# The second product of an MLP as seven block products, with sums of weight blocks made ahead

## The chip, the cores and the metric

The kernel runs on one core of a Trainium2 chip. It is written against the core's engines directly: TensorE (PE) multiplies matrices into PSUM, VectorE (DVE), ScalarE (ACT) and GpSimd (POOL) work on tiles element by element, SyncE (SP) issues the DMAs. The metric is the time of one execution on the device, in microseconds; lower is better. Times given as the median are over three runs.

## The reference

Two decoder layers over 512 tokens of 1024 features. Each layer has an attention mixer, then a squared-ReLU MLP with 4096 hidden features, then a gate from an embedding:

```python
hn = rms(h, g_mlp_pre[i])
y = jnp.square(jax.nn.relu(hn @ w_mlp_in[i])) @ w_mlp_out[i]
h = h + rms(y, g_mlp_post[i])
gate = jax.nn.sigmoid(h @ w_ple_gate[i])
h = h + gate * (p[i] @ w_ple_proj[i])
```

`hn @ w_mlp_in` is 512x1024 by 1024x4096, the product with `w_mlp_out` 512x4096 by 4096x1024, the gate 512x1024 by 1024x1024. All data is float32.

## The kernel before

Each float32 operand is split into a high part (a cast to a shorter type, by ScalarE) and a low part (what is left, by VectorE or GpSimd), and each product is three matmuls, high by high, high by low, low by high (`mm3`, L200 to 209). Weights come through one stream (`Stream`, L127 to 163): a 128x1024 piece is loaded by SyncE into `raw` (four buffers), cast into `wh` and subtracted into `wl` (four each). A piece is prepared when an earlier one is freed, and SyncE runs one queue in program order.

The code that the change touches is `layer_tail`, the MLP and gate of a layer, called once per layer:

1. The first product (`z`, L834 to 876) yields the hidden features transposed, 32 tiles `a` of 128 features by 512 tokens. Each takes 24 matmuls of 512 columns into one PSUM bank, then VectorE (into a tile with the tag `t`, which has two buffers) and ScalarE make the squared ReLU of it, scaled, in `at`.
2. The second product (`y`, L884 to 919) has eight PSUM banks, four rows of 128 tokens by two halves of 512 output features. In each of 32 rounds `k` one tile `a` is split into `ah` and `al`, and `mm3` is done for all eight banks: 24 matmuls. The last four rounds (`TAIL`) are held and then done row by row: after a row's matmuls VectorE, ScalarE and GpSimd form its norm and update the residual `h` (`post_norm`, L306), and the row before it is transposed (`pre_transpose`, `transpose_rows`, L233) for the gate.
3. The gate product (`pj` into `proj`, L251) reads these transposed rows (tiles `big`, named `hg`) and the stream's `w_g`; the low part of a transposed row is written by VectorE at L249.

The order in which each engine gets its instructions is that in which the Python code issues them, with a scheduler that may move an instruction ahead of others on its engine where no data forbids it. In the lists below a name with a number is one buffer of a tile.

Of the kernel before, what the change touches and what calls it, by code (L numbers as in the profile page):

```python
# [10 lines left out]
F32 = mybir.dt.float32  # L11
# [7 lines left out]
P = 128  # L19
# [26 lines left out]
TAIL = 4  # L46
# [12 lines left out]
def trunk_kernel(ctx, tc, A, out):  # L59
# [15 lines left out]
    def bank(tag, name):  # L75
        return psum.tile([P, 512], F32, tag=tag, name=name)
# [13 lines left out]
    def f32(ap):  # L90
        return ap.bitcast(F32)


    hspill = nc.dram_tensor("h_spill_dram", (NR, P, D), F32, kind="Internal").ap()
    ples = nc.dram_tensor("ple_dram", (2, NR, P, D), F32, kind="Internal").ap()
# [26 lines left out]
    class Stream:  # L122
# [22 lines left out]
        def load(self, upto):  # L145
            while len(self.raws) <= min(upto, len(self.specs) - 1):
                src, n, _ = self.specs[len(self.raws)]
                raw = ring.tile([P, 1024], F32, tag="raw", bufs=RAW, name="raw")
                sync.dma_start(raw[:, :n], src)
                self.raws.append(raw)  # L150
# [23 lines left out]
    for i in range(2):  # L174
# [20 lines left out]
        for j in range(KF):  # L195
            ws.add(A[f"w_mo{i}"][j], 1024)
# [615 lines left out]
    def layer_tail(i, p0, og, oT, hts, last, begin=None):  # L812
        gi = 4 * i
        with tc.tile_pool(name=f"tail{i}", bufs=1) as mp:
# [51 lines left out]
            for fb in range(NB):  # L866
                if fb:
                    z_part(*first[fb], 256, 512)
                ws.free()
                z_evac(fb, first[fb][0])  # L870
            for fb in range(NB, KF):
                h, l = ws.next()
                ps = bank("A", "z")
                z_part(ps, h, l, 0, 512)
                ws.free()
                z_evac(fb, ps)

# [6 lines left out]
            acc = [[None] * 2 for _ in range(NR)]  # L884
            for r in range(NR):
                for n in range(2):
                    acc[r][n] = bank("AB"[n], f"y{r}{n}")
            tailk = []

            def y_mm(r, n, ah, al, h, l, k):  # L890
                c = slice(r * P, (r + 1) * P)
                w = slice(n * 512, (n + 1) * 512)
                mm3(acc[r][n], ah[:, c], al[:, c], h[:, w], l[:, w], k == 0, k == KF - 1)

            for k in range(KF):
                h, l = ws.next()
                ah = mp.tile([P, S], F32R, tag="ah", bufs=5, name="ah")
                al = mp.tile([P, S], F32R, tag="al", bufs=5, name="al")
                src = at[k // 4][:, k % 4, :]
                act.copy(ah, src)  # L900
                pool.tensor_tensor(al, src, f32(ah), op=ALU.subtract)  # L901
                if k < KF - TAIL:
                    for r in range(NR):
                        for n in range(2):
                            y_mm(r, n, ah, al, h, l, k)
                    ws.free()
                else:
                    tailk.append((ah, al, h, l, k))
            new_big()
            xg = make_xt([0, 1], [2, 3], KD, f"hg{i}")  # L910
            ssy = keep(8)
            for r in range(NR):
                for ah, al, h, l, k in tailk:
                    for n in range(2):
                        y_mm(r, n, ah, al, h, l, k)
                if r:
                    pre_transpose(mp, r - 1, None, xg)
                post_norm(mp, r, acc[r], gpost, ssy)
            ws.free(TAIL)

# [13 lines left out]
            def gate0(r, ps):  # L934
                gate(r, ps, 0)
                if r == 1:
                    pre_transpose(mp, 3, None, xg)
# [16 lines left out]
            drain(proj(xg, 512, [2] * 4, range(NR), gate0))  # L954
# [337 lines left out]
```

## Time and profile before

| what | value |
|---|---|
| median of three runs | 1355.7 us (1354.56 to 1356.21) |
| the profiled execution | 1353.69 us |
| its span, first to last instruction | 1351.9 us |
| TensorE busy (matmul) | 1329.3 us, 98% |
| weight loads of TensorE | 1117.6 us, 83% |
| VectorE busy | 708.1 us, 52% |
| ScalarE busy | 574.1 us, 42% |
| GpSimd busy | 261.3 us, 19% |
| DMA | 135.39 MB, mean 100 GB/s |

Busy times of different engines overlap, so they do not add up to the span. A busy TensorE is no proof that it works at full rate: the bars of matmuls overlap in the pipeline (each is drawn longer than the time by which it advances the queue), so the rate is read from the distance between starts, or from a count over a stretch. The profile also lists a granted clock of TensorE, 1.00 at full speed.

### The profile page before, as it was taken

How to read it: one execution, taken by the hardware profiler on the slowest of the kernel's cores; microseconds unless marked ns; L12 is line 12 of the kernel's file. 1: busy time of each engine (PE TensorE's matmuls, PEld its weight loads, DVE VectorE, ACT ScalarE, POOL GpSimd, SP SyncE). 2: the span in 40 equal slices, each digit the busy share in tenths (PEclk: the TensorE clock that was granted, in tenths of full speed). 3: DMA queues.
4: the chain of work that ended last, by engine and by line, in shares of the span. 5: the costliest groups of instructions: out<-in, count | busy, mean ns of one | idle time of the engine just before them, and what ended most of it. 6: DMA issues, size and time to landing. Idle time of an engine off the chain costs nothing.

```text
span 1351.9 us, 17863 instructions
## 1 busy us (share of the span) xinstructions
PE 1329.3 (98%) x6809; PEld 1117.6 (83%) x6809; DVE 708.1 (52%) x1297; ACT 574.1 (42%) x1113; POOL 261.3 (19%) x233
## 2 busy tenths in 40 slices
PE   9999989999999999999998999999999999999998
PEld 6888878898888888888897679998988888888887
DVE  6678676473333322225568999965633332222263
ACT  4245576353322223224346768854422232222332
POOL 4212101031000022222012744411400001222120
PEclk9999989999999999999999999999999999999999
DMA  7312232333333433332243341011433334333321
GB/s 288 107 63 71 63 125 73 131 116 119 94 94 95 157 104 96 94 94 84 87 151 102 110 119 39 1 64 63 141 94 97 105 94 156 94 95 104 98 78 48
DMA packets 40838, 135.39 MB, mean 100 GB/s; under 512 B 4656, under 2 KB 5808, under 8 KB 40752
## 3 DMA queue, kind: packets, MB, share of 16 engines
q1 hardware_dynamic: 40752, 134.24, 31.1%
q8 instruction: 54, 0.88, 0.3%
q14 instruction: 32, 0.26, 0.1%
HBM read 125.83 MB, written 8.39 MB: 99 GB/s over the span
## 4 chain that ended last, share of the span: by engine, by line
PE 87%; DVE 8%; ACT 2%; POOL 1%; issue 1%; DMA 1%; SPq 0%; POOLq 0%; DVEq 0%; ACTq 0%
PE z L201 26%; PE y L201 26%; PE pj L201 21%; PE sc L201 3%; PE pv L201 3%; DVE work L1123 2%; PE trp L361 2%; DVE m L1122 2%; PE ak L201 1%; PE ple L201 1%; PE tr L242 1%; POOL wl L141 1%; DVE wl L141 1%; PE trq L381 1%; DMA xraw<-in_xT_dram 1%
## 5 line engine op out<-in xcount | busy, mean ns | idle before, releaser
L141 DVE TENSOR_TENSOR wl<-raw,wh 128x1024 fp32r<-128x1024 f32 (+3 forms) x190 | 249.1, 1316 | 276.9 <-ACT wh L137 275.1
L137 ACT CAST wh<-raw 128x1024 fp32r<-128x1024 f32 (+3 forms) x206 | 212.2, 1034 | 282.1 <-issue 184.8
L201 PE MATMUL y<-wh,ah 128*128 128x512 f32 x512 | 199.6, 390 | 0.0
L201 PE MATMUL y<-wh,al 128*128 128x512 f32 x512 | 199.2, 389 | 0.0
L201 PE MATMUL y<-wl,ah 128*128 128x512 f32 x512 | 199.2, 389 | 0.0
L201 PE MATMUL pj<-wh,big 128*128 128x512 f32 (+1 forms) x444 | 148.5, 386 | 0.0
L846 DVE SCALAR_TENSOR_TENSOR t<-z,rb 128x512 f32<-128x512 f32 x64 | 44.2, 691 | 186.9 <-PE z L201 186.9
L201 PEld LDWEIGHTS y<-wh,ah 128*128 128x128 f32 x512 | 96.1, 188 | 19.9
L201 PEld LDWEIGHTS y<-wl,ah 128*128 128x128 f32 x512 | 96.1, 188 | 19.8
L201 PEld LDWEIGHTS y<-wh,al 128*128 128x128 f32 x512 | 96.1, 188 | 19.8
L901 POOL TENSOR_TENSOR al<-big,ah 128x512 fp32r<-128x512 f32 x24 | 32.5, 1359 | 383.3 <-ACT ah L900 383.3
L201 PE MATMUL z<-hz0H,wl 128*128 128x512 f32 (+1 forms) x288 | 105.4, 366 | 0.6 <-DVE wl L141 0.6
L201 PE MATMUL z<-hz0H,wh 128*128 128x512 f32 (+1 forms) x288 | 105.5, 366 | 0.2 <-ACT hz0H L248 0.2
L201 PE MATMUL z<-hz1H,wh 128*128 128x512 f32 (+1 forms) x288 | 105.5, 366 | 0.2 <-ACT hz1H L248 0.2
L201 PE MATMUL z<-hz1L,wh 128*128 128x512 f32 (+1 forms) x288 | 105.4, 366 | 0.3 <-DVE hz1L L249 0.3
L201 PE MATMUL z<-hz0L,wh 128*128 128x512 f32 (+1 forms) x288 | 105.4, 366 | 0.3 <-DVE hz0L L249 0.3
L201 PE MATMUL z<-hz1H,wl 128*128 128x512 f32 (+1 forms) x288 | 105.3, 365 | 0.0
L201 PEld LDWEIGHTS pj<-wh,big 128*128 128x128 f32 x444 | 82.9, 188 | 17.5 <-issue 0.7
L900 ACT CAST ah<-a 128x512 fp32r<-128x512 f32 x40 | 24.8, 621 | 154.7 <-PE y L201 154.7
L901 POOL TENSOR_TENSOR al<-a,ah 128x512 fp32r<-128x512 f32 x40 | 51.7, 1292 | 165.9 <-ACT ah L900 165.9
L209 POOL TENSOR_TENSOR st<-st,mhalf 128x1 f32<-128x1 f32 (+1 forms) x41 | 27.9, 682 | 225.4 <-DVE st L312 115.6
L201 PEld LDWEIGHTS z<-hz0H,wl 128*128 128x128 f32 x288 | 54.3, 189 | 9.4 <-DVE wl L141 0.8
(598 smaller groups left out, 2640.6 us busy)
## 6 DMA issues: line engine op xcount, KB each, us to landing
raw<-in_w_mi_dram SPq DMA_DIRECT2D x64, 512.0 KB, 3.7
raw<-in_w_mo_dram SPq DMA_DIRECT2D x64, 512.0 KB, 3.6
raw<-in_w_ab_dram SPq DMA_DIRECT2D x20, 512.0 KB, 4.9
raw<-in_w_g_dram SPq DMA_DIRECT2D x16, 512.0 KB, 3.7
raw<-in_w_oab_dram SPq DMA_DIRECT2D x8, 512.0 KB, 4.3
ple<-ple_dram SPq DMA_DIRECT2D x8, 512.0 KB, 5.7
raw<-in_w_oc_dram SPq DMA_DIRECT2D x8, 512.0 KB, 3.6
xr<-in_x_dram SPq DMA_DIRECT2D x4, 512.0 KB, 9.5
```

What stands on the lines that cost most here:

```text
L137: act.copy(h[:, :n], raw[:, :n])
L141: (pool if e == "p" else vec).tensor_tensor(l[:, c], raw[:, c], f32(h[:, c]), op=ALU.subtract)
L201: pe.matmul(ps, a, b, start=first, stop=last, skip_group_check=True)
L209: pool.tensor_tensor(dst, src, mhalf[:, :n], op=ALU.pow)
L242: pe.transpose(ps[:, i * P : (i + 1) * P], src(k), ident)
L361: pe.transpose(ps[:, i * P : (i + 1) * P], pt[:, OFF[qt] + kt * P : OFF[qt] + (kt + 1) * P], ident)
L381: pe.transpose(ps[:, r * P : (r + 1) * P], rows(r), ident)
L846: vec.scalar_tensor_tensor(t, ps, 0.0, rb, op0=ALU.max, op1=ALU.mult)
L900: act.copy(ah, src)
L901: pool.tensor_tensor(al, src, f32(ah), op=ALU.subtract)
L1122: vec.max(m8, w)
L1123: vec.match_replace(w, m8, w, MARK)
```

## The change

The second product is computed on 2x2 blocks: the tokens in two halves, pairs of 128 hidden features, the outputs in two halves. Seven products of blocks (numbered 1 to 7), made of sums and differences of blocks, take the place of eight. They are done in two passes over the 16 pairs, since a product needs two PSUM banks (two rows of 128 tokens): in the first pass products 5, 7, 1 and 6, in the second 2, 3 and 4. A piece of the weight stream serves 24 matmuls in the first pass per two pieces, and 36 per three in the second.

- The sums of weight blocks are made while the first product runs (`block_sums`): four blocks of 128x512 are loaded, GpSimd subtracts four times, and four blocks are stored to a DRAM tensor `tsum`, from which the stream reads them later. This is done 16 times per layer; the tiles share the tags `ah` and `al`.
- The sums of activation blocks (`sm`, tag `t`, and in place in `a`) are made by VectorE in front of each pair, 256 columns each. The low parts of activations are now VectorE's; GpSimd made them before.
- After the first pass, ScalarE and VectorE copy and add the eight banks into tiles `d` in SBUF, so that the banks are free for the second.
- The last group of the second pass is done one half of the rows after the other. Each half then gives two rows (`r` and `r + 2`), whose norms are formed from SBUF, and four rows of transposes follow.
- The rows of the gate product are taken in the order 0, 2, 1, 3.

Line numbers of the new code lie 8 to 10 lower in the file up to the first product; L857 is the line that was L846, L142 is L141, L260 is L249, L321 to L328 are L310 to L317.

```diff
@@ -92,6 +91,8 @@
     hspill = nc.dram_tensor("h_spill_dram", (NR, P, D), F32, kind="Internal").ap()
+    tsum = nc.dram_tensor("tsum_dram", (2, KF // 2, 2, P, D), F32, kind="Internal").ap()
     ples = nc.dram_tensor("ple_dram", (2, NR, P, D), F32, kind="Internal").ap()
     ident = const.tile([P, P], F32, name="ident")
     gpre0 = const.tile([P, KD], F32, name="gpre0")
@@ -146,7 +147,11 @@
             while len(self.raws) <= min(upto, len(self.specs) - 1):
                 src, n, _ = self.specs[len(self.raws)]
                 raw = ring.tile([P, 1024], F32, tag="raw", bufs=RAW, name="raw")
-                sync.dma_start(raw[:, :n], src)
+                if isinstance(src, list):
+                    for q, piece in enumerate(src):
+                        sync.dma_start(raw[:, q * 512 : (q + 1) * 512], piece)
+                else:
+                    sync.dma_start(raw[:, :n], src)
                 self.raws.append(raw)
         def next(self):
@@ -192,8 +197,14 @@
             ws.add(A["w_oc" if i else "w_oab"][j], 1024)
         for j in range(KF):
             ws.add(A[f"w_mi{i}"][j], 1024, Z_ENG[j])
-        for j in range(KF):
-            ws.add(A[f"w_mo{i}"][j], 1024)
+        wo, lo, hi = A[f"w_mo{i}"], slice(0, 512), slice(512, 1024)
+        for j in range(KF // 2):
+            ws.add(tsum[i, j, 0], 1024)
+            ws.add([wo[2 * j][:, lo], tsum[i, j, 1][:, hi]], 1024)
+        for j in range(0, KF // 2, 2):
+            ws.add(wo[2 * j + 1], 1024)
+            ws.add([tsum[i, j + q, 1][:, lo] for q in range(2)], 1024)
+            ws.add(wo[2 * j + 3], 1024)
         for j in range(8):
             ws.add(A[f"w_g{i}"][j], 1024, G_ENG[j])
@@ -868,12 +879,30 @@
                     z_part(*first[fb], 256, 512)
                 ws.free()
                 z_evac(fb, first[fb][0])
+            def block_sums(j):
+                b = [[mp.tile([P, 512], F32, tag=("ah", "al")[q], bufs=5, name="b") for n in range(2)] for q in range(2)]
+                c = [slice(0, 512), slice(512, 1024)]
+                for q in range(2):
+                    for n in range(2):
+                        sync.dma_start(b[q][n], A[f"w_mo{i}"][2 * j + q][:, c[n]])
+                (b11, b12), (b21, b22) = b
+                for d, x, y in ((b11, b12, b11), (b12, b22, b12), (b22, b22, b11), (b21, b22, b21)):
+                    pool.tensor_tensor(d, x, y, op=ALU.subtract)
+                for q in range(2):
+                    for n in range(2):
+                        sync.dma_start(tsum[i, j, q][:, c[n]], b[q][n])
             for fb in range(NB, KF):
+                if fb % 2 == 0:
+                    block_sums(fb // 2 - 2)
                 h, l = ws.next()
                 ps = bank("A", "z")
                 z_part(ps, h, l, 0, 512)
                 ws.free()
                 z_evac(fb, ps)
+            for j in range(KF // 2 - 2, KF // 2):
+                block_sums(j)
             pls = [slot(4 + q, f"ple{q}").rearrange("p (r d) -> p r d", d=D) for q in range(2)]
             for r in range(NR):
@@ -881,42 +910,117 @@
             gpost = gtile(mp, gi + 2, "gpost2")
             gnext = None if last else gtile(mp, gi + 3, "gnext")
...
+            NP = KF // 2
+            L, R = slice(0, 256), slice(256, 512)
+            x = [[at[j // 2][:, j % 2 * 2 + q, :] for q in range(2)] for j in range(NP)]
+            def part_tiles():
+                return [mp.tile([P, S], F32R, tag=nm, bufs=5, name=nm) for nm in ("ah", "al")]
+            def split(parts, c, src):
+                h, l = parts
+                act.copy(h[:, c], src)
+                vec.tensor_tensor(l[:, c], src, f32(h[:, c]), op=ALU.subtract)
+            def banks(ps):
+                return {p: [bank("AB"[r], f"y{p}{r}") for r in range(2)] for p in ps}
+            def mul(ps, r, a, qa, w, qw, first, last):
+                ca, cw = slice(qa * 256 + r * P, qa * 256 + (r + 1) * P), slice(qw * 512, (qw + 1) * 512)
+                mm3(ps[r], a[0][:, ca], a[1][:, ca], w[0][:, cw], w[1][:, cw], first, last)
+            acc = banks((5, 7, 1, 6))
+            held = []
+            def one(j, r, ops):
+                for p, a, qa, w, qw in ops:
+                    mul(acc[p], r, a, qa, w, qw, j == 0, j == NP - 1)
+            for j in range(NP):
+                x1, x2 = x[j]
+                sm = mp.tile([P, S], F32, tag="t", bufs=2, name="sm")
+                vec.tensor_tensor(sm[:, L], x1[:, R], x2[:, R], op=ALU.add)
+                vec.tensor_tensor(sm[:, R], x1[:, L], x1[:, R], op=ALU.subtract)
+                vec.tensor_tensor(x1[:, R], sm[:, L], x1[:, L], op=ALU.subtract)
+                a, a1 = part_tiles(), part_tiles()
+                split(a, slice(0, S), sm)
+                split(a1, slice(0, S), x1)
+                w = ws.next()
+                ops = [(5, a, 0, w, 0), (7, a, 1, w, 1)]
+                if j < NP - 2:
+                    for r in (1, 0):
+                        one(j, r, ops)
+                    ws.free()
+                w = ws.next()
+                ops1 = [(1, a1, 0, w, 0), (6, a1, 1, w, 1)]
+                if j < NP - 2:
+                    for r in (1, 0):
+                        one(j, r, ops1)
                     ws.free()
                 else:
+                    held.append((j, ops + ops1))
+            dt = []
+            for r in range(2):
+                for j, ops in held:
+                    one(j, r, ops)
+                d = slot(hts[2 + r], f"d{r}")
+                dt.append([d[:, q * 512 : (q + 1) * 512] for q in range(4)])
+            for r in range(2):
+                d11, d12, d21, c22 = dt[r]
+                act.copy(d11, acc[1][r])
+                for d, b, p in ((d21, d11, 6), (d12, d21, 5), (d21, d21, 7), (c22, d21, 5)):
+                    vec.tensor_tensor(d, acc[p][r], b, op=ALU.add)
+            ws.free(4)
+            acc = banks((2, 3, 4))
+            for j in range(0, NP, 2):
+                ac, a4 = [], part_tiles()
+                for q in range(2):
+                    x1, x2 = x[j + q]
+                    vec.tensor_tensor(x1[:, R], x2[:, L], x1[:, R], op=ALU.subtract)
+                    if q == 1:
+                        split(a4, R, x1[:, R])
+                    else:
+                        split(a4, L, x1[:, R])
+                    ac.append(part_tiles())
+                    split(ac[q], slice(0, S), x2)
+                ops = []
+                w0, w4, w1 = ws.next(), ws.next(), ws.next()
+                for q, w in ((0, w0), (1, w1)):
+                    ops.append([(2, ac[q], 0, w, 0), (3, a4, q, w, 1)])
+                ops4 = [[(4, ac[q], 1, w4, q)] for q in range(2)]
+                if j == NP - 2:
+                    new_big()
+                    xg = make_xt([0, 1], [2, 3], KD, f"hg{i}")
+                    ssy = keep(8)
+                    for r in range(2):
+                        for q in range(2):
+                            one(j + q, r, ops[q])
+                        for q in range(2):
+                            one(j + q, r, ops4[q])
+                        d11, d12, d21, c22 = dt[r]
+                        vec.tensor_tensor(d11, acc[2][r], d11, op=ALU.add)
+                        vec.tensor_tensor(d12, acc[3][r], d12, op=ALU.add)
+                        post_norm(mp, r, (d11, d12), gpost, ssy)
+                        vec.tensor_tensor(d21, d21, acc[4][r], op=ALU.subtract)
+                        post_norm(mp, r + 2, (d21, c22), gpost, ssy)
+                    ws.free(3)
+                    continue
+                for r in range(2) if j == 0 else (None,):
+                    rs = range(2) if r is None else (r,)
+                    for q, o in ((0, ops[0]), (0, ops4[0]), (1, ops4[1]), (1, ops[1])):
+                        for rr in rs:
+                            one(j + q, rr, o)
+                ws.free(3)
+            for r in (0, 2):
+                pre_transpose(mp, r, None, xg)
             xn = None if last else make_xt([6, 7], [8, 9], KD, "hc")
             rn = None if last else keep(4)
@@ -933,8 +1037,8 @@
             def gate0(r, ps):
                 gate(r, ps, 0)
-                if r == 1:
-                    pre_transpose(mp, 3, None, xg)
+                if r % 2 == 0:
+                    pre_transpose(mp, 1 + r, None, xg)
             def h_next(r):
                 pre_transpose(mp, r, gnext, xn)
@@ -951,7 +1055,7 @@
                     if r:
                         h_next(r - 1)
-            drain(proj(xg, 512, [2] * 4, range(NR), gate0))
+            drain(proj(xg, 512, [2] * 4, (0, 2, 1, 3), gate0))
             drain(proj(xg, 512, [2] * 4, range(NR), gate1, halves=last))
             if last:
                 return
```

VectorE at the end of the first product of layer 0, before: `t` is the squared ReLU's first step for a tile of `z`, `wl` the low part of a weight.

```order
L141 TENSOR_TENSOR wl_3825<-raw_3691,wh_3824 128x1024
L846 SCALAR_TENSOR_TENSOR t_3864<-z_3833,rb_2829 128x512
L141 TENSOR_TENSOR wl_3859<-raw_3725,wh_3858 128x1024
L846 SCALAR_TENSOR_TENSOR t_3898<-z_3867,rb_2829 128x512
L141 TENSOR_TENSOR wl_3893<-raw_3759,wh_3892 128x1024
L141 TENSOR_TENSOR wl_3948<-raw_3793,wh_3947 128x1024
```

After: `sm` and the sum into `big_2656` (a tile `a`) are sums of activation blocks, `al` the low part of one.

```order
L857 SCALAR_TENSOR_TENSOR t_4091<-z_4060,rb_2829 128x512
L142 TENSOR_TENSOR wl_4086<-raw_3918,wh_4085 128x1024
L857 SCALAR_TENSOR_TENSOR t_4126<-z_4094,rb_2829 128x512
L949 TENSOR_TENSOR sm_4179<-big_2656 128x256
L142 TENSOR_TENSOR wl_4120<-raw_3952,wh_4119 128x1024
L950 TENSOR_TENSOR sm_4179<-big_2656 128x256
L949 TENSOR_TENSOR sm_4228<-big_2656 128x256
L951 TENSOR_TENSOR big_2656<-sm_4179,big_2656 128x256
L950 TENSOR_TENSOR sm_4228<-big_2656 128x256
L928 TENSOR_TENSOR al_4184<-sm_4179,ah_4183 128x512
```

Where low parts of weights stood alone, the sums of the first two pairs and the first activation's low part now stand between and behind the last evacuations.

VectorE between the two passes of layer 0, after the change (before, there was no such place): `d1` are the additions that take the second row half's banks out of PSUM, `al_4993` belongs to the second activation tile of the second pass.

```order
L142 TENSOR_TENSOR wl_4949<-raw_4795,wh_4948 128x1024
L142 TENSOR_TENSOR wl_4956<-raw_4813,wh_4955 128x1024
L979 TENSOR_TENSOR d1_4937<-y61_4178,d1_4937 128x512
L142 TENSOR_TENSOR wl_4962<-raw_4844,wh_4961 128x1024
L979 TENSOR_TENSOR d1_4937<-y51_4172,d1_4937 128x512
L142 TENSOR_TENSOR wl_4968<-raw_4862,wh_4967 128x1024
L979 TENSOR_TENSOR d1_4937<-y71_4174,d1_4937 128x512
L928 TENSOR_TENSOR al_4993<-big_2656,ah_4992 128x512
L979 TENSOR_TENSOR d1_4937<-y51_4172,d1_4937 128x512
```

The low part `al_4993` stands behind four low parts of weights and three additions.

VectorE at the end of the second product of layer 0, before: `yg` is the product with the norm's gain, `h0` and `h1` the residual, `big_4887<-tr` the low part of a transposed row, `wl` a weight of the gate.

```order
L310 TENSOR_TENSOR yg_5011<-y20_3915,gpost2_3907 128x512
L310 TENSOR_TENSOR yg_5011<-y21_3916,gpost2_3907 128x512
L249 TENSOR_TENSOR big_4887<-tr_4997,hg0H0_4888 128x4x128
L249 TENSOR_TENSOR big_4887<-tr_5004,big_4887 128x4x128
L312 TENSOR_SCALAR st_76<-st_76 128x1
L317 SCALAR_TENSOR_TENSOR h1_2317<-yg_5011,st_76,h1_2317 128x512 x2
L141 TENSOR_TENSOR wl_5072<-raw_4767,wh_5071 128x1024
L141 TENSOR_TENSOR wl_5078<-raw_4801,wh_5077 128x1024
L310 TENSOR_TENSOR yg_5060<-y30_3917,gpost2_3907 128x512
L310 TENSOR_TENSOR yg_5060<-y31_3918,gpost2_3907 128x512
L249 TENSOR_TENSOR big_4887<-tr_5046,hg0H0_4888 128x4x128
L249 TENSOR_TENSOR big_4887<-tr_5053,big_4887 128x4x128
```

After: `d1` are the last additions of the second row half, `big_5491<-tr_5599` is the first low part of a transposed row.

```order
L1009 TENSOR_TENSOR d1_4937<-y21_4975,d1_4937 128x512
L328 SCALAR_TENSOR_TENSOR h1_2317<-yg_5525,st_76,h1_2317 128x512 x2
L1010 TENSOR_TENSOR d1_4937<-y31_4977,d1_4937 128x512
L321 TENSOR_TENSOR yg_5556<-d1_4937,gpost2_4167 128x512 x2
L323 TENSOR_SCALAR st_76<-st_76 128x1
L1012 TENSOR_TENSOR d1_4937<-d1_4937,y41_4979 128x512
L328 SCALAR_TENSOR_TENSOR h0_2316<-yg_5556,st_76,h0_2316 128x512 x2
L321 TENSOR_TENSOR yg_5568<-d1_4937,gpost2_4167 128x512 x2
L323 TENSOR_SCALAR st_76<-st_76 128x1
L142 TENSOR_TENSOR wl_5580<-raw_5403,wh_5579 128x1024
L328 SCALAR_TENSOR_TENSOR h1_2317<-yg_5568,st_76,h1_2317 128x512 x2
L260 TENSOR_TENSOR big_5491<-tr_5599,hg0H0_5492 128x4x128
```

Before, two low parts of a transposed row stood in front of each row's update; now the first stands behind the updates of all four rows.

SyncE in the first product of layer 0, before: the loads of the weight stream.

```order
L149 DMA raw_3075<-in_w_mi0_dram 128x1024
L149 DMA raw_3109<-in_w_mi0_dram 128x1024
L149 DMA raw_3143<-in_w_mi0_dram 128x1024
L149 DMA raw_3177<-in_w_mi0_dram 128x1024
L149 DMA raw_3211<-in_w_mi0_dram 128x1024
```

After: `b` are the blocks loaded for the sums, `tsum` the stores of the results.

```order
L888 DMA b_3534<-in_w_mo0_dram 128x512
L154 DMA raw_3241<-in_w_mi0_dram 128x1024
L888 DMA b_3535<-in_w_mo0_dram 128x512
L888 DMA b_3536<-in_w_mo0_dram 128x512
L888 DMA b_3537<-in_w_mo0_dram 128x512
L888 DMA b_3618<-in_w_mo0_dram 128x512
L894 DMA tsum_dram<-b_3534 128x512
L154 DMA raw_3275<-in_w_mi0_dram 128x1024
L894 DMA tsum_dram<-b_3535 128x512
L894 DMA tsum_dram<-b_3536 128x512
L894 DMA tsum_dram<-b_3537 128x512
```

Between two weight loads there stand now loads and stores of blocks, and a store waits for GpSimd's subtraction into its tile.

## Rows read from the trace of the kernel before

**Rows 1.** page, chain that ended last, by engine and line, shares of the span
```profile
PE z L201 26%; PE y L201 26%; PE pj L201 21%; PE sc L201 3%; PE pv L201 3%; DVE work L1123 2%; PE trp L361 2%; DVE m L1122 2%; PE ak L201 1%; PE ple L201 1%; PE tr L242 1%; POOL wl L141 1%; DVE wl L141 1%; PE trq L381 1%; DMA xraw<-in_xT_dr
```

**Rows 2.** chain of waits in pieces, layer 0: start us, us, engine, tile, count
```profile
296.79 160.98 PE z L201 x744
457.77 163.20 PE y L201 x720
620.97 0.88 PE tr L242 x8
```

**Rows 3.** timeline of TensorE, end of `z`, layer 1: start us, us, what
```profile
1125.01 0.39 PE L201 MATMUL z<-hz1H,wl 128*128 128x512 f32 x1
1125.24 0.39 PE L201 MATMUL y<-wh,ah 128*128 128x512 f32 x1
```

**Rows 4.** timeline of VectorE, the same place; in brackets idle before and releaser
```profile
1125.44 0.69 DVE L846 SCALAR_TENSOR_TENSOR t<-z,rb 128x512 f32<-128x512 f32 x1 [3.31 <-PE z L201]
```

**Rows 5.** timeline of ScalarE, the same place
```profile
1125.25 1.05 ACT L137 CAST wh<-raw 128x1024 fp32r<-128x1024 f32 x1 [3.85 <-issue]
```

**Rows 6.** timeline of VectorE, last rows of `y`, layer 0
```profile
622.39 0.68 DVE L249 TENSOR_TENSOR big<-tr,hg0H 128x512 fp32r<-128x512 f32 x1
622.99 0.68 DVE L249 TENSOR_TENSOR big<-tr,big 128x512 fp32r<-128x512 f32 x1
...
624.46 0.75 DVE L317 SCALAR_TENSOR_TENSOR h<-yg,st,h 128x512 f32<-128x512 f32 x1 [0.67 <-POOL st L209]
...
632.12 2.36 DVE L141 TENSOR_TENSOR wl<-raw,wh 128x1024 fp32r<-128x1024 f32 x2
...
638.69 1.76 DVE L317 SCALAR_TENSOR_TENSOR h<-yg,st,h 128x512 f32<-128x512 f32 x1 [1.70 <-POOL st L209]
```

**Rows 7.** timeline of GpSimd, the same place
```profile
638.63 1.27 POOL L141 TENSOR_TENSOR wl<-raw,wh 128x512 fp32r<-128x512 f32 x1
```

**Rows 8.** groups by line and form: count, busy us, mean ns, idle before, releaser
```profile
L529 DVE TENSOR_TENSOR scr<-pj,cs 128x256 f32<-128x256 f32 x24 | 9.0, 414 | 0.8 <-POOL ak L530 0.8
...
L900 ACT CAST ah<-a 128x512 fp32r<-128x512 f32 x40 | 24.8, 621 | 154.7 <-PE y L201 154.7
...
L901 POOL TENSOR_TENSOR al<-big,ah 128x512 fp32r<-128x512 f32 x24 | 32.5, 1359 | 383.3 <-ACT ah L900 383.3
```

**Rows 9.** timeline of TensorE, attention of layer 0, beside the first slow clock
```profile
185.67 1.25 PE L361 MATMUL trp<-ident,pb 128*128 128x128 f32 x8 [2.07 <-DVE bk4L L384]
...
188.25 0.69 PE L361 MATMUL trp<-ident,pb 128*128 128x128 f32 x2 [1.33 <-DVE st L346]
...
189.16 0.63 PE L201 MATMUL ple<-wl,wh 128*128 128x512 f32 x1
...
189.59 0.63 PE L201 MATMUL ple<-wh,wl 128*128 128x512 f32 x1
```

**Rows 10.** windows: PE, PEld, DVE, ACT, POOL busy; TensorE clock; DMA share; GB/s
```profile
187.00:189.00 2.00, 0.75 (x3) 0.75 (x4) 1.54 (x10) 2.00 (x8) 0.00 (x0) 0.55 0.77 269
193.00:195.00 2.00, 2.00 (x15) 2.00 (x14) 1.38 (x5) 1.14 (x3) 0.00 (x0) 0.74 0.39 139
730.00:732.00 2.00, 2.00 (x6) 1.41 (x6) 2.00 (x2) 0.27 (x1) 0.45 (x1) 0.50 0.18 29
732.00:734.00 2.00, 2.00 (x12) 1.96 (x11) 0.64 (x2) 1.67 (x4) 0.00 (x0) 0.67 0.84 209
```

**Rows 11.** DMA issues: count, KB each, median us from issue to landing
```profile
ple<-ple_dram SPq DMA_DIRECT2D x8, 512.0 KB, 5.7
...
raw<-in_w_mi_dram SPq DMA_DIRECT2D x64, 512.0 KB, 3.7
...
raw<-in_w_uq_dram SPq DMA_DIRECT2D x3, 256.0 KB, 2.9
```

**Rows 12.** windows, the same columns: start of the program, `z` of layer 0
```profile
8.00:10.00 2.00, 1.90 (x8) 1.25 (x8) 1.01 (x3) 0.72 (x1) 0.00 (x0) 1.00 1.04 408
296.00:458.00 162.00, 162.00 (x753) 135.75 (x753) 60.51 (x63) 52.82 (x69) 7.22 (x5) 1.00 0.34 102
```

More of the change, by code (lines that the diff above doesn't have):

```diff
@@ L45 @@
 PRE_AV = 4
-TAIL = 4
 WARM = 10
@@ L883, in layer_tail @@
             gnext = None if last else gtile(mp, gi + 3, "gnext")
[L884 to L905, printed above, removed]
+            NP = KF // 2
@@ L906, in layer_tail @@
                     ws.free()
                 else:
[L908 to L918, printed above, removed]
@@ L919, in layer_tail @@
-            ws.free(TAIL)
+                    held.append((j, ops + ops1))
[10 more added lines that the diff above has]
+                    vec.tensor_tensor(d, acc[p][r], b, op=ALU.add)
```

## The prediction

> **What bounds the kernel now.** I read the chain of waits first, then the timelines of the two places where the second MLP product begins and ends, then the DMA views. The chain is TensorE almost throughout, and 26% of it is the line of the second product, `y` [rows 1]. In that stage 720 matmuls take 163.20 us, so one of 512 columns costs 0.2267 us however long its own bar is [rows 2]; the 768 of a layer take 174 us. So matmuls removed are time removed, as long as nothing else begins to end the waits. The seams are tight too: the first `y` matmul would come 0.23 us after the last `z` matmul [rows 3].
>
> **What is removed.** Seven block products instead of eight: per layer 2 x 16 x 7 x 3 = 672 matmuls of the same shape instead of 768, 192 fewer in the program. 192 x 0.2267 = 43.5 us, or 21.8 per layer. This part is nearly sure; what follows is what is given back.
>
> **Seam A: start of the first pass (4.2 us per layer).** Before, the weights and activations of the first round are ready when `z` ends. Now the sums of activations take the tile tag `t`, which has two buffers and also serves the evacuation of `z`, and VectorE's order has the first sum behind the last evacuation. VectorE starts that evacuation 0.2 us after TensorE's turn ends (its last matmul starts at 1125.01, VectorE at 1125.44) [rows 3, 4]. Queued back to back, VectorE takes 0.60 us per 512 columns (622.39 to 622.99) and 1.13 per 1024 (two in 2.36, whose end overlaps the next by the same 0.08 or 0.09) [rows 6]; a 256-column one lasts 0.41 [rows 8], which I take as 0.33 back to back, the same 0.08 of overlap. From the end of `z`: evacuation to 0.8, first sum to 1.1, a weight's low part to 2.3 (its cast is done at 1.1, [rows 5]), second sum to 2.7; ScalarE's cast 0.62 [rows 8] to 3.4; the load of the stationary block puts the first matmul at 3.6. The third needs the low part, which VectorE writes after three more short ops: 4.4, so 4.6 instead of 0.45. Bounds 3.4 to 5.0.
>
> **Seam B: between the passes (3.3 us per layer).** The last two rounds of pass one are held, row half 0 first, so the first half's four sums hide. But VectorE then has, in order, two low parts of weights, an evacuation, a low part, an evacuation, a low part, an evacuation, and only then the low part of the second activation tile that the twelfth matmul of pass two needs. From the point where TensorE ends pass one (the cast and copy before the first evacuation end at 0.75): 0.65 + 1.13 + 0.65 + 1.13 + 0.65 + 0.6 = 4.8, so it is there at 5.6 and TensorE, there at 2.5, goes on at 5.9. Bounds 2.0 to 4.5.
>
> **Seam C: end of the product to the gate product (10.5 us per layer).** Before, the tail ran row by row over four rows of 5.4 us each, and each row's norm and transposes lay under the next row's matmuls. Now each half ends two rows at once, in halves of 4.1 us, and VectorE's order has the low part of the first transposed row behind the norms of all four rows and one weight. TensorE's third gate matmul waits for it. VectorE's queue from the first addition: 6 additions at 0.62, 8 multiplications at 0.60, 8 updates at 0.70, 4 short ones at 0.12 (an estimate, in proportion the fixed part of a bar), one weight 1.13 = 15.8, and some 0.5 of waits for GpSimd's power, 0.67 each where nothing covers them [rows 6, 7]. It starts when product 2 of the first half is whole, 27 matmuls = 6.1 us before TensorE ends, and 0.2 later, so it ends at 10.4; 0.7 for the low part, 0.25 to the matmul: 11.4. Of this 16 transposes (0.88 per 8, [rows 2]) and two matmuls are work that is there in any case: 9.2 idle. GpSimd's three weight pieces fall into the same stretch: beside one, an update of 0.75 took 1.76 [rows 6, 7]. One or two of them hit: 10.5. Bounds 8.5 to 12.5. The Trainium skill (GPSIMD Engine Reference, 1. Specifications) says the two engines share their interfaces to SBUF and collide where VectorE reads two SBUF inputs. By that rule the multiplications collide too now, since their sources were in PSUM and are in SBUF; this trace shows it for the update alone (1.76 against 0.75), and by the rule C would lie at its upper bound.
>
> **The clock after these stalls (5.2 us per layer).** The granted clock fell twice in this trace. Once TensorE had idled 2.07 us, run 8 small transposes and idled 1.33 [rows 9]; the clock was 0.50, that is 1.2 instead of 2.4 GHz, from 187.2 to 194.0 by the means of 0.55 and 0.74 in the two stretches that hold its ends [rows 10]. Once it was 0.50 from 730 on, until 733.3 by the mean of 0.67 [rows 10]. Matmuls of 512 columns then come 0.43 us apart [rows 9], so 47% of such a stretch is lost: 1.6 to 3.2 us each time. Stall C is longer than any here, so I count it as falling for sure (2.2); A and B are as long as the stretches that made it fall, but whole: 1.7 and 1.3 with the chance in them. Bounds 1.6 (C alone, short) to 6.4.
>
> **What I cost at nothing.** Pass one: per pair VectorE has two weight parts, two activation parts, four short sums: 2.26 + 1.2 + 1.3 = 4.8 of TensorE's 5.44; GpSimd's `al` work (1.36 beside it) is gone from there. With less cover, 0 to 1.5 us per layer. Pass two: 5.3 of 8.16. The 64 GpSimd subtractions per layer at 1.36 [rows 8] are 87 us under 161 us of `z`; the chain that feeds them is the second rival.
>
> **Sum.** Per layer -21.8 + 4.2 + 3.3 + 10.5 + 5.2 = +1.4; twice, +2.9. The profiled execution took 1353.69 (span 1351.9 and 1.8 around it), so it would take 1356.6; the median shown lies 2.0 above that execution, so 1358.6.
>
> **Rivals.**
> 1. Not slower: the clock holds in A and B and the stalls lie at their lower bounds. The queue that makes C is certain, but A and B end on single ops that I chained by hand, and both falls in this trace came after ragged stretches, not one clean gap. Then -21.8 + 3.4 + 2.0 + 8.5 + 1.6 = -6.3 per layer: 1343; with middle stalls and only C's fall, -21.8 + 18.0 + 2.2 = -1.6: 1352.5. It decides at idle plus clock below 21.8 us per layer.
> 2. Much slower: the loads of `z`'s own weights come late. SyncE is one queue in order. Now each block's four loads and four stores stand between those loads, and a store at the head waits for GpSimd. One block takes 2.9 to land 256 KB, 0.8 for a second piece behind it (3.7 for 512 KB) [rows 11], 4 x 1.36 and 0.5 of issue: 9.6 us, three of them per five weight loads, 29 us against 27.2 of TensorE. Over 24 loads that is 8 us late, and eight tiles of lead are 40. But the DMAs carry 48 MB in `z` instead of 16: share 0.34 at 102 GB/s becomes nearly 1.0 at that rate, though 408 GB/s has been seen [rows 12]. If pieces land at 5.7 us, as the 512 KB of `ple` do [rows 11], a block takes 12.5, the lag is 50 us, and TensorE waits some 10 us per layer: 1379. The Trainium skill (DMA: Bandwidth & Descriptors, Measured) asks for 1 MiB per DMA and gives 341 GB/s there and 138 at 64 KB; our 256 KB pieces would by an estimate between them get some 240 GB/s, and 48 MB would take 200 us, more than `z` has. The 408 GB/s of [rows 12], moved in pieces of 512 KB, speaks against it.
> 3. The gain stays: TensorE finds its operands, as in every round of the product now. Against it stand three fixed orders of VectorE. Then 1355.7 - 43.5 = 1312 at best, 1333 with C alone, its 10.5 twice.
> 4. VectorE becomes the bound in pass one: 4.8 of 5.44 leaves little. At 5.8 per pair it costs 16 x 0.36 = 5.8 us per layer on top of the forecast: 1370.
>
> **How the numbers follow.** Forecast 0.45, rival 1 0.22, rival 2 0.18, rival 3 0.10, rival 4 0.05. The forecast's own range is 1354 to 1366. What this kernel's measurement can tell from no change is 0.2%, 2.7 us: 1353.0 to 1358.4. The forecast's case splits 0.17 same, 0.28 slower; rival 1 0.14 faster, 0.08 same; rival 2 slower; rival 3 faster; rival 4 0.02 same, 0.03 slower. So faster 0.24, same 0.27, slower 0.49. The bounds of all costs, with the 0 to 1.5 of pass one, give -6.3 to +8.1 per layer, 1343 to 1372; with part of rival 2 above and the lowest corner and rival 3 left out, 1346 to 1374.
>
> **What would show it.** In the profile after: 192 fewer `y` matmuls at the same 0.2267 us; an idle TensorE of 3 to 5 us at the start of pass one with VectorE's line of sums and then ScalarE's split as its releasers, one of 2 to 4 us eleven matmuls into pass two, and one of 8 to 12 us between the transposes and the gate product, released by VectorE's line that writes the low part; a granted clock of 0.5 behind the last, and in some layer behind the others. `z` should keep its 161 us for 744 matmuls; if it is longer and TensorE waits there for casts that wait for DMAs, rival 2 is true. The forecast is wrong at its root if TensorE shows no wait at C, or if the half clock does not come after it.

## The result, and the profile after

| | kernel before | changed kernel |
|---|---|---|
| median | 1355.13 us (4 runs, 1353.2 to 1356.21) | 1421.59 us (4 runs, 1415.13 to 1423.22) |
| profiled execution, span | 1353.69, 1351.9 us | 1415.13, 1413.3 us |
| granted clock, mean | 0.996 | 0.971 |

The ratio is 1.0483, 95% interval [1.0447, 1.0519]: slower by 66 us, where 2.9 were forecast. The sign was right, but not for the forecast's reason; the size was not, and the time lies outside the range.

The changed kernel's chain, by engine and line, answers to [rows 1]:

```profile
PE y L212 20%; PE pj L212 11%; PE z L212 7%; DMA b<-in_w_mo_dram 7%; POOL b L891 6%; PE sc L212 2%; PE pv L212 2%; DVE work L1227 2%; DVE wl L142 2%; DMA raw<-tsum_dram 2%; DVE m L1226 2%; DMA raw<-in_w_mi_dram 1%; PE trp L372 1%; ACT wh L138 1%; SPq L894 1%
```

`z` was 26% of the chain and is 7%. In its place stand the loads of blocks, GpSimd's subtractions and the loads from `tsum`: in the first product the end is no longer set by TensorE. What TensorE waited for in the changed kernel (us in total, times, longest):

```profile
PE y L212 <- ACT ah L927: 32.4, 2, 16.8
PE pj L212 <- DVE big L260: 21.5, 2, 10.8
PE z L212 <- DVE wl L142: 13.4, 13, 1.3
PE z L212 <- ACT wh L138: 10.7, 8, 3.2
PE y L212 <- DVE al L928: 5.1, 2, 2.6
```

The three seams of the forecast are there, in rows 1, 5 and 2: A at the start of `y`, B between the passes, C in front of the gate product. B is 2.6 a layer and C 10.8, as forecast (3.3 and 10.5). A is 16.8 instead of 4.2, and the two rows of `z` are new. TensorE's timeline at the end of `z` in layer 0, to compare with [rows 3], where 0.23 us lay between the two products:

```profile
472.86 0.39 PE L212 MATMUL z<-hz0H,wl 128*128 128x512 f32 x1
490.03 0.80 PE L212 MATMUL y<-wh,ah 128*128 128x512 f32 x1 [16.79 <-ACT ah L927]
```

From the first matmul of `z` to the first of `y` it took 179.6 us before (278.0 to 457.6) and now 213.5 (276.5 to 490.0): 33.9 more. That is nearly the whole miss: twice 33.9, less the 4.2 forecast for A in each layer, is 59. Half of it lies in `z` itself, which took 196.6 us instead of 179.6: 12.1 of waits for its own weights, and most of the rest from a clock of 0.50 between 447.7 and 453.5. The other half is the wait of 16.8 at the start of `y`. Of the path to 490.03, the chain of waits shows its parts (start us, us, what):

```profile
467.39 5.44 DMA raw<-tsum_dram
...
472.94 1.05 ACT wh L138
...
474.01 2.17 DVE wl L142
...
477.46 7.02 DMA raw<-tsum_dram
...
486.80 0.68 DVE t L857
```

The first weights of `y` are loaded at 467 and 477, when `z` is over or nearly so, since they stand in SyncE's queue behind stores of the sums (the first behind all but the last three, the second behind all). The last weight of `z` itself was issued at 461.8, behind 58 of the 64 stores, 5.7 us after `z` would have ended at its old length. And VectorE has a low part of such a weight in front of `z`'s last evacuation (486.80), which so comes 13.7 us after `z`'s end at 473.1. SyncE's queue in layer 0, the first block's loads and the last block's stores:

```profile
282.93 1.14 SPq L888 DMA_DIRECT2D b<-in_w_mo_dram  x2
...
472.40 3.03 SPq L894 DMA_DIRECT2D tsum_dram<-b  x3
```

Sixteen blocks take 282.9 to 475.4, 12.0 us each. One of them in the chain:

```profile
344.49 4.65 DMA b<-in_w_mo_dram
...
349.27 2.08 POOL b L891
...
354.12 0.33 SPq L894
...
355.45 5.00 DMA b<-in_w_mo_dram
```

Landing of the last piece, then three subtractions (2.08, 1.29 and 1.30; the first of the four ran at 346.30, ahead of that landing), then two stores and a load, 1.3 us of issues, and only then the next block's last load. Of the next block only the first two loads were issued earlier, at 347.98. So this block takes 11.0 us. From last load to last load the others take 10.9 to 12.9: landings took up to 6.1 (453.86 to 459.94), and the issues took 2.4 where three loads of the next block and a weight load of `z` stand behind the stores (378.3 to 380.7).

The subtraction of 2.08 ran beside a low part of VectorE:

```profile
348.98 1.23 DVE L142 TENSOR_TENSOR wl<-raw,wh 128x1024 fp32r<-128x1024 f32 x1 [0.88 <-ACT wh L138]
349.27 2.08 POOL L891 TENSOR_TENSOR b<-b 128x512 f32<-128x512 f32 x1 [1.69 <-DMA b<-in_w_mo_dram]
```

Of the 128 subtractions 35 took 1.56 to 2.30 us, every one of them beside a `wl`; the 60 that met no `wl` took 1.27 to 1.30. In the same way a `wl`, 1.22 alone, took up to 2.28 beside one.

The account of layer 0, first matmul of `z` to the same point of layer 1 (668.6 us before, 701.2 now): 96 matmuls less, -21.8; `y` begins 33.9 later; clock at 0.50 after that until 494.8, at 47% of its time 2.3; B 2.6; C 0.7 and 10.8; clock after C until 665.5, 1.7. The sum is +30.2 of a measured +32.6. The 2.4 left are about what the clock takes in layer 1's attention, where it was 0.50 three times (754 to 758, 792 to 795 and 840 to 843) and in the kernel before once (730 to 733): 3.2 by the same 47%. Why it falls there is open.

### The profile page after: what moved, and what is told of

It reads as the page before. It is cut to its first block, busy times and chain, and to the rows that moved or that the text cites. A ratio compares the mean times of both kernels' runs of the same rounds, so it can differ in the third digit from the quotient of the medians.

```text
span 1413.3 us, 18830 instructions
## 1 busy us (share of the span) xinstructions
PE 1308.6 (93%) x6617; PEld 1090.2 (77%) x6617; DVE 902.5 (64%) x1629; ACT 654.0 (46%) x1229; POOL 371.6 (26%) x297
## 2 busy tenths in 40 slices
DMA packets 91535, 227.74 MB, mean 161 GB/s; under 512 B 10288, under 2 KB 11440, under 8 KB 91440
## 4 chain that ended last, share of the span: by engine, by line
PE 46%; DMA 10%; DVE 9%; POOL 7%; issue 3%; SPq 2%; ACT 2%; POOLq 0%; ACTq 0%; DVEq 0%
PE y L212 20%; PE pj L212 11%; PE z L212 7%; DMA b<-in_w_mo_dram 7%; POOL b L891 6%; PE sc L212 2%; PE pv L212 2%; DVE work L1227 2%; DVE wl L142 2%; DMA raw<-tsum_dram 2%; DVE m L1226 2%; DMA raw<-in_w_mi_dram 1%; PE trp L372 1%; ACT wh L138 1%; SPq L894 1%
## 5 line engine op out<-in xcount | busy, mean ns | idle before, releaser
L142 DVE TENSOR_TENSOR wl<-raw,wh 128x1024 fp32r<-128x1024 f32 (+3 forms) x238 | 312.7, 1318 | 279.0 <-ACT wh L138 276.5
L138 ACT CAST wh<-raw 128x1024 fp32r<-128x1024 f32 (+3 forms) x254 | 262.0, 1035 | 389.6 <-DMA raw<-in_w_mi_dram 201.6
L891 POOL TENSOR_TENSOR b<-b 128x512 f32<-128x512 f32 x128 | 193.1, 1512 | 181.1 <-DMA b<-in_w_mo_dram 170.8
L212 PE MATMUL y<-wh,ah 128*128 128x512 f32 x448 | 176.4, 394 | 32.4 <-ACT ah L927 32.4
L212 PE MATMUL y<-wh,al 128*128 128x512 f32 x448 | 176.1, 393 | 5.1 <-DVE al L928 5.1
L212 PE MATMUL y<-wl,ah 128*128 128x512 f32 x448 | 175.9, 393 | 0.0
L212 PE MATMUL pj<-wh,big 128*128 128x512 f32 (+1 forms) x444 | 150.2, 390 | 21.5 <-DVE big L260 21.5
L212 PEld LDWEIGHTS y<-wh,ah 128*128 128x128 f32 x448 | 85.2, 190 | 50.8 <-ACT ah L927 33.2
L212 PEld LDWEIGHTS pj<-wh,big 128*128 128x128 f32 x444 | 83.6, 190 | 40.3 <-DVE big L260 22.4
L212 PE MATMUL z<-hz1H,wl 128*128 128x512 f32 (+1 forms) x288 | 107.2, 372 | 7.5 <-DVE wl L142 7.5
L212 PE MATMUL z<-hz0H,wh 128*128 128x512 f32 (+1 forms) x288 | 107.2, 372 | 6.5 <-ACT wh L138 6.2
L212 PE MATMUL z<-hz0H,wl 128*128 128x512 f32 (+1 forms) x288 | 107.3, 372 | 5.9 <-DVE wl L142 5.9
L212 PE MATMUL z<-hz1H,wh 128*128 128x512 f32 (+1 forms) x288 | 107.2, 372 | 4.7 <-ACT wh L138 4.5
L212 PE MATMUL z<-hz1L,wh 128*128 128x512 f32 (+1 forms) x288 | 106.6, 370 | 0.3 <-DVE hz1L L260 0.3
L212 PE MATMUL z<-hz0L,wh 128*128 128x512 f32 (+1 forms) x288 | 106.4, 369 | 0.3 <-DVE hz0L L260 0.3
L212 PEld LDWEIGHTS y<-wh,al 128*128 128x128 f32 x448 | 85.0, 190 | 24.4 <-DVE al L928 6.8
L212 PEld LDWEIGHTS y<-wl,ah 128*128 128x128 f32 x448 | 85.2, 190 | 17.6
L857 DVE SCALAR_TENSOR_TENSOR t<-z,rb 128x512 f32<-128x512 f32 x64 | 43.8, 684 | 46.2 <-PE z L212 46.2
L212 PEld LDWEIGHTS z<-hz1H,wl 128*128 128x128 f32 x288 | 55.1, 191 | 19.1 <-DVE wl L142 10.3
L212 PEld LDWEIGHTS z<-hz0H,wl 128*128 128x128 f32 x288 | 55.0, 191 | 17.5 <-DVE wl L142 8.6
L212 PEld LDWEIGHTS z<-hz0H,wh 128*128 128x128 f32 x288 | 55.0, 191 | 16.9 <-ACT wh L138 7.9
```

Of the source, the lines that this page charges most:

```text
L138: act.copy(h[:, :n], raw[:, :n])
L142: (pool if e == "p" else vec).tensor_tensor(l[:, c], raw[:, c], f32(h[:, c]), op=ALU.subtract)
L212: pe.matmul(ps, a, b, start=first, stop=last, skip_group_check=True)
L857: vec.scalar_tensor_tensor(t, ps, 0.0, rb, op0=ALU.max, op1=ALU.mult)
L891: pool.tensor_tensor(d, x, y, op=ALU.subtract)
```

## Experiments

Each kernel ran beside the kernel before on the same chip; that took 1351.59 us in the first four (one execution), 1354.36 in e5 to e7 and 1353.57 in e8 and e9 (medians). e1 to e4 and e9 are one execution each themselves. Since the kernel before took 2.8 us less beside e4 than beside e5 to e7, the gains over e4 named below are by that much larger when each is taken against its own neighbour.

**e1: the block products without the sums of blocks.**

```diff
-            ws.add(tsum[i, j, 0], 1024)
...
+            ws.add(wo[2 * j + 1], 1024)
...
-                    block_sums(fb // 2 - 2)
+                    pass
...
```

Expected: 

> Leaves out the sums of weight blocks (their loads, subtractions and stores); the second product reads unsummed pieces of w_mlp_out of the same sizes, so its output is another. Queue theory and traffic theory alike: z goes back from 177 to about 161 us per layer and the wait at the start of y from 16 to about 4; what is left is the forecast's own sum, about 1357 us for an execution (1346 to 1364). If seams A, B and C were mis-sized themselves, it lies outside that.

Measured: 1359.69 us. `y` waits 3.2 us at its start, B 2.6, C 10.8:

```profile
PE pj L212 <- DVE big L260: 21.5, 2, 10.8
PE y L212 <- ACT ah L927: 6.5, 2, 3.2
PE y L212 <- DVE al L928: 5.4, 3, 2.6
```

So the forecast's own sum (1358.6) describes the seven products without the making of their weights; the other 60 us belong to the sums. Against the kernel before beside it e1 is 8.1 slower, where 2.9 was forecast. Most of the difference, 4.4 us, is a clock of 0.50 in layer 1's attention (726 to 737 and 812 to 819), for 12.8 us of work where the kernel before has 3.4; the forecast had no term for that.

**e9: the sums without the block products** (the kernel before, with `block_sums` in `z` and its result unused).

Expected: 

> The kernel before with the sums of weight blocks added in z, as in the changed kernel, and not used. Queue theory: z takes 177 us instead of 161, and the first weights of y come late behind the last stores by 5 to 13 us: 1352 becomes 1392 to 1410. If the seven block products were part of what slows z, less: under 1385.

Measured: 1422.84 us, 69 more than before, above the expected range of 1392 to 1410. TensorE waits in `z` for its own last weights, up to 21.4 us at once:

```profile
PE z L202 <- ACT wh L138: 46.1, 6, 21.4
PE z L202 <- DVE wl L142: 9.0, 10, 1.3
```

From the first matmul of `z` to the first of `y`, layer 0 takes 213.8 us here (276.7 to 490.5) and 213.5 in the changed kernel, where the kernel before takes 179.6; twice 34.2 is 68 of the 69. The seven products have no part in that loss. That e1's 8 and e9's 69 do not add up to 66 fits this: `y` begins no later with seam A than without it, so while TensorE waits for late weights, seam A's work is done beside it.

**e2: the same bytes without the wait.**

```diff
-                        sync.dma_start(tsum[i, j, q][:, c[n]], b[q][n])
+                        sync.dma_start(tsum[i, j, q][:, c[n]], rb)
```

Expected: 

> The stores read a tile written long before instead of the sums (so the stored values are others); loads, subtractions, stores and bytes stay the same, only SyncE's wait for GpSimd goes. Queue theory (each block's loads stand behind the stores of the block before, 11 us a block): z back to 161 to 165 us, execution 1355 to 1368. Traffic theory (48 MB in z make the transfers late): z stays near 177, execution 1405 to 1420.

Measured: 1353.18 us. All loads, subtractions and stores are there (128 of each, 227.74 MB in all as in the changed kernel), and `z` has its old length (276.0 to 455.6). The traffic theory falls. `rb` is a tile written long before, so the output is another.

**e4: the loads one block ahead.** The same instructions, in another order:

```diff
+            def block_loads(j):
...
             def block_sums(j):
+                block_loads(j + 1)
...
+            block_loads(0)
```

Expected: 

> Same instructions, but each block's loads are issued one block ahead, in front of the stores of the block before. Queue theory: a block's period falls from 11.1 us to what GpSimd and the stores need, 7 to 9 us, z 161 to 168, execution 1357 to 1375. Traffic theory: 1410 to 1420.

Measured: 1357.59 us, 64 less than the changed kernel's median. SyncE's queue, layer 0, at the first load, and the last stores with the first load for `y` in front of them:

```profile
283.51 0.42 SPq L891 DMA_DIRECT2D b<-in_w_mo_dram  x1
...
421.89 0.32 SPq L154 DMA_DIRECT2D raw<-tsum_dram  x1
422.30 2.90 SPq L902 DMA_DIRECT2D tsum_dram<-b  x3
```

A block takes 8.9 us (283.5 to 425.2, 16 blocks) instead of 12.0, though its pieces land later. The issues of the changed kernel, and then of e4 (count, KB, median us to landing):

```profile
b<-in_w_mo_dram SPq DMA_DIRECT2D x128, 256.0 KB, 4.6
tsum_dram<-b SPq DMA_DIRECT2D x128, 256.0 KB, 2.4
```

```profile
b<-in_w_mo_dram SPq DMA_DIRECT2D x128, 256.0 KB, 5.6
tsum_dram<-b SPq DMA_DIRECT2D x128, 256.0 KB, 5.7
```

**e3: the stores issued by GpSimd** (`pool.dma_start` in place of `sync.dma_start`).

Expected: 

> The stores are issued by GpSimd behind its own subtractions instead of by SyncE; same bytes. Queue theory: z 161 to 168, execution 1355 to 1372, if GpSimd's issues are short. Traffic theory: no change, 1410 to 1420. If the issue of a store costs GpSimd more than 1 us, 16 blocks take over 9 us each on it and the end of the sums comes late at the start of y instead.

Measured: 1404.66 us, a miss of both theories' numbers as written. GpSimd is not the bound: an issue takes it 0.56 us and a block 8. But the scheduler, seeing no stores on SyncE, put four or five block loads in front of each weight load of `z`, and those wait until the store of an earlier block has landed and its buffer is free (176 us in all, by the list of waits of SyncE's queue):

```profile
340.60 5.03 SPq L888 DMA_DIRECT2D b<-in_w_mo_dram  x4
345.71 0.38 SPq L154 DMA_DIRECT2D raw<-in_w_mi_dram  x1
347.33 7.63 SPq L888 DMA_DIRECT2D b<-in_w_mo_dram  x5
355.08 0.38 SPq L154 DMA_DIRECT2D raw<-in_w_mi_dram  x1
```

Here one weight load comes in 9.4 us, where TensorE uses one in 5.44. `z` waits again, and `y` does not (6.6 us in two layers, as in e1). By the trace it is the same cause, a queue in order, with another instruction at its head; no run takes that instruction away.

**e5: seam C, the order of norms** (on top of e4).

```diff
                         vec.tensor_tensor(d12, acc[3][r], d12, op=ALU.add)
+                        if r:
+                            for q in (0, 2):
+                                pre_transpose(mp, q, None, xg)
                         post_norm(mp, r, (d11, d12), gpost, ssy)
...
-            for r in (0, 2):
-                pre_transpose(mp, r, None, xg)
```

The transposes of rows 1 and 3 are also moved from the ends of rows 0 and 2 of the gate product into the middles of rows 2 and 1.

Expected: 

> On top of e4_loads_ahead: the transposes of rows 0 and 2 are asked for ahead of the norms of rows 1 and 3, and those of rows 1 and 3 in the middle of the gate product. Theory of seam C (VectorE's queue stands between, 10.8 us idle and some 1.5 us of half clock per layer): 1357.6 falls by 14 to 24, to 1334 to 1344. Rival (the wait is for GpSimd's power and its weight pieces, which the order does not change): under 6 us gained, 1352 or more.

Measured: 1353.64 us (ratio to before 0.9988 [0.9977, 0.9998]), 4 less than e4's one execution: near the rival's number, but not for its reason. The wait of 10.8 for the transposed row is gone, and one of 7.2 for a weight of the gate took its place (`PE pj L212 <- DVE wl L142: 14.5, 2, 7.2` in its list).

**e6: seam A, a tile of its own for the sums** (on top of e4).

```diff
-                sm = mp.tile([P, S], F32, tag="t", bufs=2, name="sm")
+                sm = mp.tile([P, D], F32, tag="yg", bufs=2, name="sm")[:, :S]
```

Expected: 

> On top of e4_loads_ahead: the sums of activations lie in the tile of the norm instead of that of z's evacuation, so VectorE can make the first ones while z runs. Theory of seam A (3.5 us idle and 1.6 us of half clock per layer come from that shared tile): 1357.6 falls by 7 to 11, to 1347 to 1351. Rival (the first weights of y are late in any case, since their sums were stored last): no gain, 1355 to 1359.

Measured: 1344.53 us (0.9928 [0.9911, 0.9945]), 13 less than e4, somewhat more than the 7 to 11 expected. The wait at the start of `y` is gone: in the window 296 to 458 TensorE is busy all 162.00 us, in e4 160.75.

**e7: e5 and e6 together, the second pass's first split ahead of the additions that empty the banks, six buffers of `ah` and `al`** (on top of e4).

Expected: 

> On top of e4_loads_ahead: e5 and e6 together, the first activations of the second pass split before the banks of the first are taken out, and six buffers of ah and al instead of five. If the waits of A, B and C and the half clock behind them (33 + 9 us in two layers) are all that is given back: 1317 to 1328, faster than before by 2 to 3%. If the gain turns into other waits (the norms' tail, GpSimd's weight pieces): 1330 to 1345.

Measured: 1333.15 us (0.9843 [0.9828, 0.9858]), in the second of its two ranges: the waits of A and B are gone, that of the gate weight is the one left. VectorE and ScalarE in e7, layer 0:

```profile
606.29 1.05 ACT L138 CAST wh<-raw 128x1024 fp32r<-128x1024 f32 x1 [1.20 <-issue]
```

```profile
616.12 2.41 DVE L328 SCALAR_TENSOR_TENSOR h<-yg,st,h 128x512 f32<-128x512 f32 x2
...
619.77 1.21 DVE L142 TENSOR_TENSOR wl<-raw,wh 128x1024 fp32r<-128x1024 f32 x1
```

The cast was done at 607.3; the low part is written at 619.8, since the code frees the buffers of the last group, and so asks for the next weights, behind the norms.

**e8: the weights asked for ahead of the norms** (on top of e7).

```diff
                         if r:
+                            ws.free(3)
                             for q in (0, 2):
                                 pre_transpose(mp, q, None, xg)
...
-                    ws.free(3)
                     continue
```

Expected: 

> On top of e7_all: the gate's second to fourth weight pieces are asked for ahead of the norms of rows 1 and 3 instead of behind them. In e7_all TensorE waits 7.2 us per layer for the low part of the second piece, whose cast was done 12 us earlier. If that place in VectorE's queue is all, 1333 falls by 12 to 18 (two waits of 7.2 and the half clock behind them), to 1315 to 1321. If the pieces made by GpSimd are late next, by 4 to 8: 1325 to 1329.

Measured: 1323.23 us (5 runs, 1319.35 to 1325.07), ratio to the kernel before 0.9774 [0.9757, 0.979]: faster by 30 us than before and by 98 than the changed kernel, and between the two ranges expected. What TensorE still waits for there:

```profile
PE tr L253 <- DVE h L328: 5.5, 4, 1.7
PE pj L212 <- DVE big L260: 2.6, 2, 1.7
```

Of the 43.5 us of matmuls some 30 are kept; the rest goes to these 8 and to what was not looked into.

## Why the prediction was wrong

- **What is removed** held: 192 matmuls fewer (6617 instead of 6809 on TensorE), at 0.2267 us where nothing waits.
- **Seams B and C** held: 2.6 for 3.3, and 10.8 with 0.7 in front for 10.5. VectorE's queue of norms stood in front of the first low part as chained. e5, e7 and e8 show that the order alone made C, GpSimd's contention only its size: two updates took 3.41 us beside GpSimd's pieces and 1.41 alone.

```profile
648.54 1.41 DVE L328 SCALAR_TENSOR_TENSOR h<-yg,st,h 128x512 f32<-128x512 f32 x2
...
657.85 3.41 DVE L328 SCALAR_TENSOR_TENSOR h<-yg,st,h 128x512 f32<-128x512 f32 x2 [0.44 <-POOL st L220]
657.79 4.61 POOL L142 TENSOR_TENSOR wl<-raw,wh 128x512 fp32r<-128x512 f32 x3
661.19 0.68 DVE L260 TENSOR_TENSOR big<-tr,hg0H 128x512 fp32r<-128x512 f32 x1
```

  Three updates were hit, for 3.0 us where 1.3 was counted. Whether the multiplications collide too, as the rule of the Trainium skill (GPSIMD Engine Reference, 1. Specifications) has it, no run shows; none fell beside a piece. But "for the update alone" was too narrow a reading: `wl`, which also reads two tiles in SBUF, takes 1.22 alone and up to 2.33 beside GpSimd, in the kernel before as well, and there the trace agrees with the rule. The evacuation of `z`, with one source in PSUM, took 0.68 to 0.69 either way. The forecast did not apply this to GpSimd's 64 subtractions, priced at 1.36 each.
- **Seam A** held where weights are there in time (3.2 in e1 for 4.2). In the changed kernel it is 16.8, for a reason that belongs to rival 2.
- **The clock** fell to 0.50 behind A and C in the changed kernel and behind all three in e4, for some 3 to 5 us each: 4.0 per layer in the account above, forecast 5.2.
- **The step that failed is rival 2's**: "Over 24 loads that is 8 us late, and eight tiles of lead are 40", and with it the chance of 0.18 and the 10 us per layer of its worse case. Its mechanism is what happened, and its sign came: `z` is longer, and TensorE waits there for casts that wait for DMAs. Three things in the sum were wrong.
  - The price of a block: 9.6 came to 12.0 in the mean. The last load landed after 4.65 (in the block shown) to 6.1 instead of 3.7, and the queue's own issues between subtraction and next load took 1.3 to 2.4 instead of 0.5. The subtractions took 4.8 instead of 5.4, but only since three of the four lie behind the landing; 0.8 of that comes from VectorE's low part.
  - The lead: 31 and not 40. The blocks stand in the queue from 282.9, 6.4 us after `z`'s first matmul, and the last piece needed 5.8 from its issue to its use (461.8 to 467.6); both go off eight tiles of 5.44. The issues of the 24 loads took from 282.9 to 461.8, 179 us, where TensorE uses 24 pieces in 131: 48 late, 17 more than the lead. `z` became 17.0 longer.
  - The loads for `y`, which the sum left out: they stand behind the last blocks in the same queue. At 9.6 the blocks end at 437, in time; at 12.0 at 475, 19 us after `z` could end (456.1), with a load of 7, low parts and the split still to come. `y` so waits another 16.8, where seam A's 4.2 was forecast.

  The forecast's own bound of 12.5 for a block, put into that sum, would have given 483, 8 us later than came and so a loss of the order measured. The price was bounded; what it does to the end was not.
- **The traffic**, which rival 2 leaned on and the Trainium skill's page (DMA: Bandwidth & Descriptors, Measured) spoke for by an estimate of 240 GB/s, was not the cause; late landings are 1 to 2.4 us of the price of a block. The trace does not agree with that estimate, which came from a table for DMAs issued by GpSimd, while these are SyncE's: in e4 the same bytes move at 304 GB/s in 256 KB and 512 KB pieces, and `z` is as long as before. The window 296 to 458 in e4, beside [rows 12] (PE, PEld, DVE, ACT, POOL busy; clock; DMA share; GB/s):

```profile
296.00:458.00 162.00, 160.75 (x743) 134.23 (x741) 68.44 (x65) 50.30 (x65) 92.97 (x60) 1.00 0.88 304
```

## What to carry to other kernels

Where loads and stores of a side job share one DMA queue with the main stream, multiply the whole chain of one piece (landing, work, store, issues) by the number of pieces and set the sum against the stage, and look who stands behind the last piece: a lead of buffered tiles helps only those in front. Then issue the loads of a piece ahead of the stores of the one before; here that alone was worth some 60 us. And after each wait that an order explains, read the order for the next late instruction: C became a wait for a weight, and only both edits together gave the gain.

## What the runs showed of the hardware

- DMA engines at a share of 0.88 and pieces landing after 5.6 instead of 2.9 us (256 KB) cost TensorE nothing in `z`, as long as nothing waited in order behind them (e4, e6). The 2.9 are of three loads in the kernel before, [rows 11].
- GpSimd's subtraction of 128x512 took 1.27 to 1.30 us where it met no low part of VectorE (two sources in SBUF), and up to 2.30 beside one, 1.51 in the mean; whichever of the two began second took longer (in layer 0: 2.08 for GpSimd at 349.27, 2.00 for VectorE at 372.41 instead of 1.22). Beside VectorE's evacuation of `z`, with one source in PSUM, it kept its 1.29.
